# A sparse-attention decoder layer on one core: value compression's add moved to ScalarE, other PSUM banks for the v tiles, two loads moved in the program

## The chip, the core and the metric

The kernel runs on one core of one Trainium2 chip. The core has a matrix engine (TensorE, in the profile PE, with its weight loads as PEld), a vector engine (VectorE, DVE), an activation engine (ScalarE, ACT), a general engine (GpSimd, POOL) and an engine that issues transfers (SyncE, SP). Each works through its own instructions in the order in which they stand, and they meet at semaphores. The metric is the time of one run on the device, in microseconds (us); less is better.

## What is computed

One decoder layer on 1024 tokens of width 1024, in float32: a mixer with eight sparse-attention heads (two key/value heads) and eight gMLP groups, then a SwiGLU block. What matters here is the compressed branch of the attention. Overlapping blocks of 32 tokens get a position added and go through a small two-layer network; the change touches this for the values:

```python
def compress_tokens(t, pos_emb, w1, w2):
    ...
    blocks = jnp.concatenate([chunks[:, :, i:i + n_cmp] for i in range(r)], axis=3)
    blocks = (blocks + pos_emb).reshape(B, G, n_cmp, CMP_BLOCK * dh)
    return jax.nn.gelu(blocks @ w1) @ w2
...
kc = compress_tokens(heads_kv(k_c), cmp_pos_k, cmp_w1_k, cmp_w2_k)
vc = compress_tokens(heads_kv(v_c), cmp_pos_v, cmp_w1_v, cmp_w2_v)
...
mixed = jnp.concatenate([nsa_out, gm.astype(h.dtype)], axis=-1)
return jnp.einsum("bse,ed->bsd", mixed, w_out)
```

The softmax uses `exp`, the small network `gelu`; `gm` is the output of the gMLP groups, which the output projection `w_out` reads beside the attention's output.

## The kernel before

Every float32 product is made of three matmuls in a rounded format: an operand is kept as a high part (`...h`, `whi`, `bh`) and a low part (the rest, `...l`, `wlo`, `bl`), and `mm3` (L182 to L185) adds high x high, high x low and low x high. So each operand costs a rounding copy and a subtraction before TensorE may read it.

The program runs in stages: input norm and gMLP (to about 165 us of the span), projections of q, k and v with the two compressions (to about 263 us), attention over eight tiles of 128 queries, from tile 7 down to tile 0, in each of which four pairs of heads are worked on and the previous tile's output projection is slipped in (to about 590 us), then SwiGLU, whose products are nearly all matmul (to the end).

Around the change, one after the other in the program:

- `compress_in` (L414) transposes the positions into `posT` (L418, L420), makes the 16 high parts `bh` (L426) and the 16 low parts `bl` (L427), all on VectorE, from the projected values `U`, and adds up 48 matmuls in PSUM tile `ps_p` (L435), three for each of 16 slices. ScalarE applies gelu (L438) and leaves `chid`. `compress_out` (L441) transposes `chid`, splits it into `chidT`, multiplies by the second weights into `ps_p` again and leaves `vch` (L464 on ScalarE, L465 on VectorE).
- `v_proj` (L482) makes the eight tiles of v and of the gates, 24 matmuls of 280 columns each; ScalarE (L489) and VectorE (L490, L491) then empty the PSUM tile. Its bank is chosen by `turn("vproj", "wpt")`: the tiles come in the program as 4, 5, 6, 7, 0, 1, 2, 3 and get w, p, t, w, p, t, w, p. There is one bank each of w, x and p, two of a and three of t. Bank p is that of the compression too.
- Between them `wo_early` (L523) loads five 512 KB pieces of `w_out` by SP and splits them (L167 on ScalarE, L173 on VectorE). The bias table `B` (1.1 MB, L508) is loaded into the space of `bh` and `bl`, so after the last compression matmul; the 20 small `qr` loads (L571, q of a pair of heads, split by POOL at L171 and L173) follow it on SP.
- In the attention, logits of a pair of heads go to banks a and x (L673, L674), VectorE adds the bias and takes the minimum (L678, L682), ScalarE applies exp (L721).
- `output_proj` (L595) reads `gmh`, the gMLP output of a tile in its two parts: two loads of 256 KB issued by POOL (L601) from `gm_scr`, which the gMLP stage wrote long before. There is one buffer.

The instructions are not put in order by hand: a scheduler orders each engine's list by its own estimate of times and by priorities (`tc.high_priority`), within what data, buffers and banks allow. A change of a bank or of an engine so moves instructions in its neighbourhood.

Of the kernel before, what the change touches and what calls it, by code (L numbers as in the profile page):

```python
# [10 lines left out]
F32R = mybir.dt.float32r  # L11
BF16 = mybir.dt.bfloat16
AF = mybir.ActivationFunctionType
ALU = mybir.AluOpType
# [3 lines left out]
P = 128  # L18
# [8 lines left out]
NCMP = 63  # L27
# [43 lines left out]
def trunk_kernel(ctx, tc, x, rel_bias, norm_mix_pre, norm_mix_post, norm_ffn_pre, norm_ffn_post, w_in,  # L71
# [3 lines left out]
    nc = tc.nc  # L75
    x = x[0]
    out = out[0]
# [7 lines left out]
    def close(g):  # L85
        if isinstance(g, Ring):
            for p, _ in g.stack[::-1]:
                close(p)
        else:
            g.__exit__(None, None, None)  # L90
# [22 lines left out]
    def turn(key, tags):  # L113
        n = turns.get(key, 0)
        turns[key] = n + 1
        return bank(tags[n % len(tags)])

    def bank(tag):
        return psp[tag][1].tile([P, 512], F32, name="ps_" + tag)
# [15 lines left out]
    act_warm = const.tile([P, 1], F32, name="act_warm")  # L135
# [5 lines left out]
    def fl(ap):  # L141
        return ap.bitcast(F32)
# [39 lines left out]
    def mm3(ps, sh, sl, mh, ml, first, last):  # L182
        nc.tensor.matmul(ps, sh, mh, start=first, stop=False)  # L183
        nc.tensor.matmul(ps, sh, ml, start=False, stop=False)  # L184
        nc.tensor.matmul(ps, sl, mh, start=False, stop=last)  # L185

    q_scr = dram.tile([H, DH, S], F32, name="q_scr")
    gm_scr = dram.tile([2, NT, P, 4, P], F32, name="gm_scr")
# [18 lines left out]
    def xT(t):  # L207
        ts = slice((t % 4) * P, (t % 4 + 1) * P)
        return xh[t // 4][:, :, ts], xl[t // 4][:, :, ts]
# [161 lines left out]
    ps = bank("p")  # L371
# [21 lines left out]
    bh = bhlpool.tile([P, 16, G, 64], F32R, name="bh")  # L393
# [17 lines left out]
                nc.vector.tensor_tensor(kt_[g][64:128, cs], src, fl(kt_[g][0:64, cs]), op=ALU.subtract)  # L411
        return f

    def compress_in(w1, pos):  # L414
        pn = cmpool.tile([16, P], F32, name="pos_nat", bufs=2)
        nc.scalar.dma_start(out=pn, in_=pos[0].rearrange("(kt jj) d -> kt (jj d)", jj=2))
        ps = bank("t")
        nc.tensor.transpose(ps[:, :16], pn, ident[:16, :16])  # L418
        posT = cmpool.tile([P, 16], F32, name="posT", bufs=2)
        nc.vector.tensor_copy(posT, ps[:, :16])  # L420
        nc.gpsimd.memset(bh[:, :, :, 63:64].bitcast(F32), 0.0)
        nc.gpsimd.memset(bl[:, :, :, 63:64].bitcast(F32), 0.0)
        uv = U.rearrange("p g (n j) -> p g n j", j=16)
        for kt in range(16):
            src = uv[:, :, kt // 8:kt // 8 + NCMP, 2 * (kt % 8)]
            nc.vector.tensor_scalar(bh[:, kt, :, :NCMP], src, posT[:, kt:kt + 1], None, op0=ALU.add)  # L426
            nc.vector.scalar_tensor_tensor(bl[:, kt, :, :NCMP], src, posT[:, kt:kt + 1], fl(bh[:, kt, :, :NCMP]),  # L427
                                           op0=ALU.add, op1=ALU.subtract)
        w1v = w1[0].rearrange("(kt p) c -> p kt c", p=P)
        ps = bank("p")  # L430
        for q4 in range(4):
            h_, l_ = wload(w1v[:, 4 * q4:4 * q4 + 4, :])
            for c in range(4):
                kt = 4 * q4 + c
                mm3(ps[:, :256], bh[:, kt].rearrange("p a b -> p (a b)"), bl[:, kt].rearrange("p a b -> p (a b)"),  # L435
                    h_[:, c, :], l_[:, c, :], kt == 0, kt == 15)
        hid = cmpool.tile([P, 256], F32, name="chid", bufs=1)
        nc.scalar.activation(hid, ps[:, :256], AF.Gelu_apprx_tanh)  # L438
        return hid

    def compress_out(hid, w2, which):  # L441
        ps = bank("t")
        for c in range(2):
            nc.tensor.transpose(ps[:, c * P:(c + 1) * P], hid[:, c * P:(c + 1) * P], ident)
        hT = cmpool.tile([P, 2, 2, P], F32R, name="chidT", bufs=1)
        split(hT[:, 0], hT[:, 1], ps[:, :256].rearrange("p (a b) -> p a b", b=P))
        w2r = cmpool.tile([P, 2, DH], F32, name="w2r", bufs=1)
        nc.scalar.dma_start(out=w2r, in_=w2[0].rearrange("(k p) d -> p k d", p=P))
        w2s = cmpool.tile([P, 2, 2, DH], F32R, name="w2s", bufs=1)
        split(w2s[:, 0], w2s[:, 1], w2r)  # L450
        ps = bank("p")
        if which == "k":
            for c in range(2):
                mm3(ps[:64, :P], w2s[:, 0, c, :], w2s[:, 1, c, :], hT[:, 0, c, :], hT[:, 1, c, :], c == 0, c == 1)
            for g in range(G):
                src = ps[0:64, 64 * g:64 * g + 64]
                nc.scalar.copy(kt_[g][0:64, 0:64], src)
                nc.vector.tensor_tensor(kt_[g][64:128, 0:64], src, fl(kt_[g][0:64, 0:64]), op=ALU.subtract)
        else:
            for c in range(2):  # L460
                mm3(ps[:, :DH], hT[:, 0, c, :], hT[:, 1, c, :], w2s[:, 0, c, :], w2s[:, 1, c, :], c == 0, c == 1)
            for g in range(G):
                src = ps[64 * g:64 * g + 64, 0:DH]
                nc.scalar.copy(vch[0:64, g, 0:DH], src)  # L464
                nc.vector.tensor_tensor(vch[0:64, g, DH:], src, fl(vch[0:64, g, 0:DH]), op=ALU.subtract)  # L465
# [15 lines left out]

    def v_proj(vw, tiles):  # L482
        for t in tiles:
            ps = turn("vproj", "wpt")
            for k in range(KD):
                mm3(ps[:, :280], xT(t)[0][:, k, :], xT(t)[1][:, k, :], vw[k][0], vw[k][1], k == 0, k == KD - 1)
            src = ps[:, :256].rearrange("p (a d) -> p a d", d=DH)
            dst = vt[:, t].rearrange("p b g c -> p (b g) c")
            nc.scalar.copy(dst[:, :, 0:DH], src)  # L489
            nc.vector.tensor_tensor(dst[:, :, DH:], src, fl(dst[:, :, 0:DH]), op=ALU.subtract)  # L490
            nc.vector.tensor_copy(gates[:, t, :], ps[:, 256:280])  # L491
# [4 lines left out]
    proj_t(C_VC, evac_u)  # L496
    compress_out(chk, cmp_w2_k, "k")
    proj_t(C_KW, evac_k(64 + S))
    chv = compress_in(cmp_w1_v, cmp_pos_v)
    close(g_bhl)  # L500
    g_bc, bcp = pool("bc", 1, "right")
    B = bcp.tile([P, H, BW], F32, name="B")
# [27 lines left out]
            wo[k] = (hi, lo)  # L530

    v_proj(vw, (4,))
    compress_out(chv, cmp_w2_v, "v")
    v_proj(vw, (5,))
    wo_early(2)
    v_proj(vw, (6,))
# [15 lines left out]
    at = {}  # L552
# [24 lines left out]
    TILES = [7, 6, 5, 4, 3, 2, 1, 0]  # L577
# [14 lines left out]
    WO0, WO1, WON, WOE = 1, 5, 2, nc.gpsimd  # L592
    PRE = (1, 1)

    def output_proj(i):  # L595
        mixh, mixl = wout_args.pop(i)
        if not bc:
            load_bc()
        gmh = at["late"].tile([P, 2, 4, P], F32R, name="gmh", bufs=1)
        for hl in range(2):  # L600
            nc.gpsimd.dma_start(out=gmh[:, hl], in_=gm_scr[hl, i])  # L601
        xt = at["late"].tile([P, D], F32, name="xt", tag="xt", bufs=1)
        nc.sync.dma_start(out=xt, in_=x[i * P:(i + 1) * P, :])
        s2 = small.tile([P, 2], F32, name="s2o")
        h1 = at["late"].tile([P, D], F32, name="h1", tag="h1", bufs=1)
        for nh in range(2):
            ps = bank("w") if i > LX else turn("opj", "wx")
            cs = slice(nh * 512, (nh + 1) * 512)
            for k in range(KD):
                kk = (k + 4) % 8  # L610
                sh, sl = (mixh[:, kk], mixl[:, kk]) if kk < 4 else (gmh[:, 0, kk - 4], gmh[:, 1, kk - 4])
                mm3(ps, sh, sl, wo[kk][0][:, cs], wo[kk][1][:, cs], k == 0, k == KD - 1)
            nc.scalar.activation(h1[:, cs], ps, AF.Square, accum_out=s2[:, nh:nh + 1])
            nc.scalar.copy(h1[:, cs], ps)
        ss = small.tile([P, 1], F32, name="ss")
        nc.vector.tensor_tensor(ss, s2[:, 0:1], s2[:, 1:2], op=ALU.add)
        r = rstd_of(ss, D, RMS_EPS)
        for nh in range(2):
            cs = slice(nh * 512, (nh + 1) * 512)
            nc.vector.scalar_tensor_tensor(h1[:, cs], h1[:, cs], r, bc["post"][:, cs], op0=ALU.mult, op1=ALU.mult)  # L620
            nc.vector.tensor_tensor(h1[:, cs], h1[:, cs], xt[:, cs], op=ALU.add)
        nc.sync.dma_start(out=h1_scr[i], in_=h1)
        return h1, xt
# [15 lines left out]
    for ti, i in enumerate(TILES):  # L639
# [5 lines left out]
        for g in range(G):  # L645
            for pr in range(2):
                if (g, pr) == OPJ and ti > 0:
                    with tc.high_priority(HO):
                        pend = output_proj(TILES[ti - 1])
                if (g, pr) == PRE and ti > 0:  # L650
                    with tc.high_priority(HF):
                        pre_ffn(TILES[ti - 1], *pend)
# [9 lines left out]
                with tc.high_priority(HP0 if at_ < 4 else HP if i >= 4 else HP2):  # L662
                    for hh in range(2):
# [23 lines left out]
                        for c0, c1 in A_CHUNKS[i]:  # L687
                            ps = logits(c0, c1)
# [15 lines left out]
                        for c0, c1 in wch:  # L704
                            ps = logits(w0 + c0, w0 + c1)
# [14 lines left out]
                        for br, (c0, c1, col) in enumerate(((0, 64, 0), (64, na, scol), (na, na + nw, wcol))):  # L720
# [6 lines left out]
                                               op0=ALU.max, op1=ALU.mult)  # L727
                nc.vector.reciprocal(wts, wts)  # L728
                with tc.high_priority(HS):
                    for br, (c0, c1) in enumerate(((0, 64), (64, na), (na, na + nw))):  # L730
                        for hh in range(2):
                            nc.gpsimd.tensor_scalar(pts[hh][:, c0:c1], pts[hh][:, c0:c1], wts[:, hh, br:br + 1], 1.0,  # L732
                                                    op0=ALU.mult, op1=ALU.mult)
                with tc.high_priority(HV):
# [4 lines left out]
                    for gi, grp in enumerate(groups):  # L739
                        wd = 256 * len(grp)  # L740
                        ps = bank("t")
# [471 lines left out]
```

## Time and profile before

| | us |
|---|---|
| median of 3 runs | 1246.94 (1246.73 to 1247.27) |
| the profiled execution, its own time | 1244.0 |
| its span in the trace | 1242.3 |
| TensorE busy | 1195.7, 96% of the span |
| VectorE, ScalarE, GpSimd busy | 913.2, 567.2, 382.5 |

The profile shows one execution. Busy time of TensorE counts a matmul from its start to its modelled end, and matmuls overlap; how fast the stream goes is read from the distance between the starts of neighbours. Where TensorE is late, the table of waits names the engine whose signal came last. The granted clock (PEclk) is a share of full speed: 1.00 is 2.4 GHz, 0.50 is 1.2 GHz, and a value between is a stretch that had some of both.

### The profile page before, as it was taken

The page shows a single profiled execution, that of the slowest core. Times are in us where ns is not written, and L with a number is a line of the kernel's source. Part 1 is how long each engine was busy: PE and PEld are TensorE (multiplying, and loading weights), DVE is VectorE, ACT ScalarE, POOL GpSimd, SP SyncE. Part 2 cuts the span into 40 slices and gives each one's busy share as a digit, 9 for nine tenths or more (in the row PEclk, how much of TensorE's full clock was granted, in tenths as well). Part 3 has the DMA queues.
Part 4 walks back from the last instruction along what each step waited for, and adds up shares of the span by engine and source line. Part 5 has one row for each costly group of instructions (what it writes and reads, how often), then busy time and mean ns, then how long its engine had stood idle before and what let it go on. Part 6 is the DMA issues. An engine that isn't in the chain of part 4 may idle for free. (4 is left out here: it accounts for less than half of the span.)

```text
span 1242.3 us, 18159 instructions
## 1 busy us (share of the span) xinstructions
PE 1195.7 (96%) x6074; PEld 1006.9 (81%) x6074; DVE 913.2 (74%) x2037; ACT 567.2 (46%) x1254; POOL 382.5 (31%) x454
## 2 busy tenths in 40 slices
PE   6999999889999999998999999999999999999997
PEld 5888878778888988886777888888888888888885
DVE  5656337659898896877589878776787747588996
ACT  4423021257777886876544332233332324544452
POOL 3315112146545545561070222210222201132341
PEclk9999999999999999999999999999999999999999
DMA  7313454331021222425404323323233189332335
GB/s 251 95 57 96 136 170 126 104 96 35 27 64 46 63 69 68 146 71 159 156 34 150 108 104 128 111 77 110 96 117 127 62 292 348 121 111 86 96 117 203
DMA packets 106229, 143.86 MB, mean 116 GB/s; under 512 B 8120, under 2 KB 64792, under 8 KB 106136
## 3 DMA queue, kind: packets, MB, share of 16 engines
q1 hardware_dynamic: 99552, 133.43, 32.8%
q0 software_dynamic: 2304, 4.20, 1.2%
q10 hardware_dynamic: 4280, 5.08, 1.2%
q8 instruction: 48, 0.79, 0.3%
q14 instruction: 45, 0.37, 0.1%
HBM read 103.60 MB, written 40.71 MB: 116 GB/s over the span
## 5 line engine op out<-in xcount | busy, mean ns | idle before, releaser
L732 POOL TENSOR_SCALAR L<-L,wts 128x64 f32<-128x64 f32 (+8 forms) x192 | 108.4, 589 | 97.6 <-DVE wts L728 61.3
L966 DVE TENSOR_TENSOR cc<-fb,cc 128x512 f32<-128x512 f32 x140 | 94.2, 686 | 55.2 <-PE fb L185 54.5
L721 ACT ACTIVATE L<-L,mm 128x64 f32<-128x64 f32 (+8 forms) x192 | 116.3, 608 | 26.6 <-DVE mm L678 26.1
L847 POOL TENSOR_TENSOR cc<-sil 128x512 f32<-128x512 f32 x22 | 35.2, 1599 | 287.9 <-issue 225.6
L173 DVE TENSOR_TENSOR pl<-ps_t,ph 128x512 fp32r<-128x512 f32 (+1 forms) x160 | 100.6, 643 | 12.7 <-ACT ph L167 11.3
L167 ACT CAST op<-s 128x512 fp32r<-128x512 f32 x80 | 49.5, 622 | 120.9 <-PE fb L185 105.8
L184 PE MATMUL fb<-wdo,hido 128*128 128x512 f32 x264 | 102.7, 389 | 0.0
L183 PE MATMUL fb<-wdo,hido 128*128 128x512 f32 x264 | 101.9, 389 | 0.0
L185 PE MATMUL fb<-wdo,hido 128*128 128x512 f32 x264 | 100.4, 389 | 0.0
L184 PE MATMUL fb<-b_b,op 128*128 128x512 f32 x256 | 99.6, 389 | 0.0
L185 PE MATMUL fb<-b_b,op 128*128 128x512 f32 x256 | 99.4, 389 | 0.0
L183 PE MATMUL fb<-b_b,op 128*128 128x512 f32 x256 | 99.3, 389 | 0.0
L167 ACT CAST ph<-ps_t 128x512 fp32r<-128x512 f32 (+1 forms) x160 | 85.0, 555 | 30.8 <-PE ps_t L744 16.4
L744 PE MATMUL ps_t<-ident,L 128*128 128x128 f32 x592 | 89.6, 275 | 4.8 <-DVE pl L173 3.9
L173 DVE TENSOR_TENSOR hido<-hidr,hido 128x512 fp32r<-128x512 f32 x77 | 60.9, 801 | 27.8 <-ACT hido L167 27.7
L744 PEld LDWEIGHTS ps_t<-ident,L 128*128 128x128 f32 x592 | 69.1, 141 | 14.3 <-issue 5.3
L167 ACT CAST hido<-hidr 128x512 fp32r<-128x512 f32 x77 | 47.4, 620 | 66.8 <-DMA hidr<-hid_scr 25.5
L1045 POOL TENSOR_TENSOR tt<-wdr 128x512 f32<-128x512 f32 x22 | 36.1, 1646 | 134.6 <-DVE wdo L173 80.0
L167 ACT CAST op<-wraw 128x512 fp32r<-128x512 f32 x60 | 37.1, 622 | 84.9 <-PE fb L185 73.7
L173 DVE TENSOR_TENSOR op<-s,op 128x512 fp32r<-128x512 f32 x80 | 63.8, 803 | 14.1 <-ACT op L167 13.4
L753 PE MATMUL ps_p<-pl,vt 128*128 128x256 f32 x264 | 73.3, 303 | 0.5 <-DVE pl L173 0.5
L751 PE MATMUL ps_p<-ph,vt 128*128 128x256 f32 x264 | 68.5, 283 | 0.0
(399 smaller groups left out, 3466.0 us busy)
## 6 DMA issues: line engine op xcount, KB each, us to landing
wraw<-in_w_gate_up_dram SPq DMA_DIRECT2D x40, 512.0 KB, 3.6
hidr<-hid_scr SPq DMA_DIRECT2D x77, 256.0 KB, 2.7
hid_scr<-sil SPq DMA_DIRECT2D x44, 256.0 KB, 2.0
wdr<-in_w_down_dram SPq DMA_DIRECT2D x44, 256.0 KB, 5.2
hid_scr<-cc SPq DMA_DIRECT2D x33, 256.0 KB, 2.1
xt<-in_x_dram SPq DMA_DIRECT2D x16, 512.0 KB, 3.7
raw<-in_w_in_dram SPq DMA_DIRECT2D x16, 512.0 KB, 4.4
gm_scr<-gmt SPq DMA_DIRECT2D x16, 256.0 KB, 2.6
```

The costliest lines, as they stand in the source:

```text
L167: nc.scalar.copy(hi, src)
L173: e.tensor_tensor(lo, src, fl(hi), op=ALU.subtract)
L183: nc.tensor.matmul(ps, sh, mh, start=first, stop=False)
L184: nc.tensor.matmul(ps, sh, ml, start=False, stop=False)
L185: nc.tensor.matmul(ps, sl, mh, start=False, stop=last)
L721: nc.scalar.activation(L[:, c0:c1], L[:, c0:c1], AF.Exp, bias=mm[:, col:col + 1], scale=-1.0, accum_out=sums[:, hh, br:br + 1])
L732: nc.gpsimd.tensor_scalar(pts[hh][:, c0:c1], pts[hh][:, c0:c1], wts[:, hh, br:br + 1], 1.0, op0=ALU.mult, op1=ALU.mult)
L744: nc.tensor.transpose(ps[:, (bi * 2 + hh) * P:(bi * 2 + hh + 1) * P], pts[hh][:, c0:c0 + P], ident)
L751: nc.tensor.matmul(pv[:, :256], v, ph[:, bi * 256:(bi + 1) * 256], start=(gi == 0 and bi == 0), stop=False)
L753: nc.tensor.matmul(pv[:, :256], v, pl[:, bi * 256:(bi + 1) * 256], start=False, stop=last)
L966: nc.vector.tensor_tensor(dst, ps, y_, op=ALU.add)
L1045: eng.tensor_tensor(dst, x_, y_, op=op)
```

## The change

Four edits. The high parts of the value compression's operand are made by ScalarE, as an activation that adds the position (`Identity` with a bias), and no more by VectorE; the key compression stays as it was. Right behind that compression a one-column `exp` is put on ScalarE, on a spare tile. The v tiles get the banks w, t, t, x, w, t, t, p in turn, and the second half of the value compression a higher priority. The loads of `gmh` stand further ahead in the program: the first before the attention, each next one behind the output projection that used the buffer.

```diff
-    def compress_in(w1, pos):
+    def compress_in(w1, pos, on_act=False):
...
         for kt in range(16):
             src = uv[:, :, kt // 8:kt // 8 + NCMP, 2 * (kt % 8)]
-            nc.vector.tensor_scalar(bh[:, kt, :, :NCMP], src, posT[:, kt:kt + 1], None, op0=ALU.add)
+            if on_act:
+                nc.scalar.activation(bh[:, kt, :, :NCMP], src, AF.Identity, bias=posT[:, kt:kt + 1])
+            else:
+                nc.vector.tensor_scalar(bh[:, kt, :, :NCMP], src, posT[:, kt:kt + 1], None, op0=ALU.add)
...
-            ps = turn("vproj", "wpt")
+            ps = turn("vproj", "wttxwttp")
...
-    chv = compress_in(cmp_w1_v, cmp_pos_v)
+    chv = compress_in(cmp_w1_v, cmp_pos_v, True)
+    nc.scalar.activation(act_warm, chv[:, 0:1], AF.Exp)
...
-    compress_out(chv, cmp_w2_v, "v")
+    with tc.high_priority(200):
+        compress_out(chv, cmp_w2_v, "v")
...
+    gms = {}
+
+    def load_gm(i):
+        gms[i] = at["late"].tile([P, 2, 4, P], F32R, name="gmh", bufs=1)
+        for hl in range(2):
+            nc.gpsimd.dma_start(out=gms[i][:, hl], in_=gm_scr[hl, i])
+
+    load_gm(TILES[0])
+
     def output_proj(i):
...
-        gmh = at["late"].tile([P, 2, 4, P], F32R, name="gmh", bufs=1)
-        for hl in range(2):
-            nc.gpsimd.dma_start(out=gmh[:, hl], in_=gm_scr[hl, i])
+        gmh = gms.pop(i)
...
                     with tc.high_priority(HO):
                         pend = output_proj(TILES[ti - 1])
+                        load_gm(i)
```

VectorE's list from the positions of the value compression on, before (`kt_1421`, `kt_1422` are the keys of the two heads, `ps_x` the bank of the last key projection):

```order
L420 COPY posT<-ps_t 128x16
L426 TENSOR_SCALAR bh<-U,posT 128x2x63 x6
L427 SCALAR_TENSOR_TENSOR bl<-U,posT,bh 128x2x63
L426 TENSOR_SCALAR bh<-U,posT 128x2x63
L427 SCALAR_TENSOR_TENSOR bl<-U,posT,bh 128x2x63
L411 TENSOR_TENSOR kt_1421<-ps_x,kt_1421 64x512
```

and after (L430 is before's L427, L493 its L490):

```order
L420 COPY posT<-ps_t 128x16
L173 TENSOR_TENSOR wlo<-raw,whi 128x1024
L411 TENSOR_TENSOR kt_1421<-ps_x,kt_1421 64x512
L430 SCALAR_TENSOR_TENSOR bl<-U,posT,bh 128x2x63 x16
L411 TENSOR_TENSOR kt_1422<-ps_x,kt_1422 64x512
L493 TENSOR_TENSOR vt<-ps_w,vt 128x4x64
```

The sixteen `bh` have left the list, the sixteen `bl` stand together, and a split of `w_out` and one key copy now stand ahead of them, the second key copy behind them.

ScalarE's list over the same place, before:

```order
L410 CAST kt_1421<-ps_x 64x512
L489 CAST vt<-ps_w 128x4x64
L410 CAST kt_1422<-ps_x 64x512
L167 CAST whi<-raw 128x1024
L489 CAST vt<-ps_w 128x4x64
L167 CAST whi<-raw 128x1024
L438 ACTIVATE chid<-ps_p 128x256
```

and after (L441 is before's L438):

```order
L410 CAST kt_1421<-ps_x 64x512
L427 ACTIVATE bh<-U,posT 128x2x63 x16
L410 CAST kt_1422<-ps_x 64x512
L492 CAST vt<-ps_w 128x4x64
L167 CAST whi<-raw 128x1024 x2
L441 ACTIVATE chid<-ps_p 128x256
L510 DMA MW<-in_window_edge_dram 128x128
L503 ACT_TABLE_LOAD
L503 ACTIVATE act_warm<-chid 128x1
L492 CAST vt<-ps_x 128x4x64
L167 CAST chidT<-ps_t 128x256
```

The sixteen `bh` come ahead of everything that empties the v tiles, and the load of the exponential's table, which before stands ahead of the attention's first exp (L721), now stands right behind gelu.

TensorE's list where the second half of the compression is over (`xTh_155` and `xTl_156` belong to tiles 4 to 7, `xTh_150` and `xTl_151` to tiles 0 to 3), before:

```order
L184 MATMUL ps_t<-wlo,xTh_150 128x280
L185 MATMUL ps_t<-whi,xTl_151 128x280
L185 MATMUL ps_w<-whi,xTl_151 128x280
L183 MATMUL ps_p<-whi,xTh_155 128x280
L184 MATMUL ps_p<-wlo,xTh_155 128x280
```

and after:

```order
L184 MATMUL ps_t<-wlo,xTh_155 128x280
L185 MATMUL ps_t<-whi,xTl_156 128x280
L184 MATMUL ps_w<-wlo,xTh_150 128x280
L185 MATMUL ps_w<-whi,xTl_151 128x280
L183 MATMUL ps_w<-whi,xTh_150 128x280
```

Before, a tile in bank p (tile 5) follows here; after, tile 0 in bank w. Bank p then comes up for tile 3 alone, the last one, with nearly all logits of the first pair of heads ahead of it.

POOL's list at the first load of `gmh`, before:

```order
L171 TENSOR_SCALAR qt<-qr 128x256
L601 DMA gmh<-gm_scr 128x512 x2
L173 TENSOR_TENSOR qt<-qr,qt 128x256
L161 TENSOR_SCALAR whi<-wo_raw 128x1024
L732 TENSOR_SCALAR L<-L,wts 128x64 x2
```

and after (L605 is before's L601, L745 its L732):

```order
L171 TENSOR_SCALAR qt<-qr 128x256
L605 DMA gmh<-gm_scr 128x512 x2
L173 TENSOR_TENSOR qt<-qr,qt 128x256
L161 TENSOR_SCALAR whi<-wo_raw 128x1024
L745 TENSOR_SCALAR L<-L,wts 128x64 x2
```

Nothing has moved: all eight pairs of these loads stand at the same place of POOL's list as before. On SP the one difference is that `B` stands ahead of the fourth piece of `w_out`, which before went ahead of it. In the first products of SwiGLU some matmuls and splits change places as well; from the attention's second pair of heads to there the lists are the same row by row.

## Rows read from the trace of the kernel before

**Rows 1.** The page's first part: busy us (share of span) of each engine.
```profile
PE 1195.7 (96%) x6074; PEld 1006.9 (81%) x6074; DVE 913.2 (74%) x2037; ACT 567.2 (46%) x1254; POOL 382.5 (31%) x454
```

**Rows 2.** Busy time by stretch; the first line names the columns.
```profile
core 0: us, PE busy (x) PEld busy (x) DVE busy (x) ACT busy (x) POOL busy (x), PEclk, DMA share, GB/s
700.00:800.00 100.00, 100.00 (x443) 82.81 (x442) 78.80 (x112) 32.79 (x55) 17.12 (x11) 1.00 0.29 99
...
217.57:263.20 45.63, 39.61 (x270) 36.76 (x269) 27.58 (x88) 14.99 (x30) 5.23 (x9) 0.96 0.24 76
...
246.00:252.00 6.00, 5.50 (x29) 5.47 (x30) 1.33 (x8) 0.74 (x3) 1.51 (x3) 0.72 0.20 56
270.00:276.00 6.00, 5.04 (x24) 4.72 (x25) 2.42 (x9) 2.93 (x8) 6.00 (x6) 0.72 0.26 77
...
650.00:660.00 10.00, 7.66 (x31) 5.56 (x31) 10.00 (x14) 4.72 (x8) 3.20 (x2) 1.00 0.68 201
```

**Rows 3.** Waits of TensorE from 217 to 264 us: total, times, longest.
```profile
PE ps_p L183 <- DVE vch L465: 2.4, 1, 2.4
PE ps_p L185 <- DVE bl L427: 1.7, 5, 0.9
PE ps_p L183 <- DVE gates L491: 1.0, 1, 1.0
```

**Rows 4.** TensorE in order of time: start, duration, instruction [idle before <-releaser].
```profile
220.80 0.28 PE L183 MATMUL ps_p<-whi,bh 128*128 128x256 f32 x1
...
227.55 0.28 PE L183 MATMUL ps_p<-whi,bh 128*128 128x256 f32 x1
...
228.74 0.28 PE L184 MATMUL ps_p<-wlo,bh 128*128 128x256 f32 x1
...
246.50 0.36 PE L183 MATMUL ps_p<-whi,xTh 128*128 128x280 f32 x1 [2.45 <-DVE vch L465]
...
250.24 0.72 PE L673 MATMUL ps_a<-kt,qt 128*128 128x448 f32 x2
...
259.99 0.29 PE L184 MATMUL ps_p<-wlo,xTh 128*128 128x280 f32 x1
...
262.57 0.30 PE L183 MATMUL ps_p<-whi,xTh 128*128 128x280 f32 x1
...
263.20 0.37 PE L673 MATMUL ps_a<-kt,qt 128*128 128x448 f32 x1
...
270.96 0.71 PE L183 MATMUL ps_w<-whi,gmh 128*128 128x512 f32 x1 [2.23 <-DMA gmh<-gm_scr]
```

**Rows 5.** ScalarE in order of time.
```profile
218.30 0.57 ACT L410 CAST kt<-ps_x 64x512 fp32r<-64x512 f32 x1
...
242.47 1.05 ACT L167 CAST whi<-raw 128x1024 fp32r<-128x1024 f32 x1 [4.97 <-DMA raw<-in_w_out_dram]
...
252.13 1.28 ACT L721 ACT_TABLE_LOAD   x1 [5.37 <-issue]
...
255.32 1.15 ACT L721 ACTIVATE L<-L,mm 128x1024 f32<-128x1024 f32 x1 [0.33 <-DVE mm L678]
...
258.89 0.35 ACT L721 ACTIVATE L<-L,mm 128x64 f32<-128x64 f32 x1
```

**Rows 6.** VectorE in order of time.
```profile
220.75 0.68 DVE L411 TENSOR_TENSOR kt<-ps_x,kt 64x512 fp32r<-64x512 f32 x1
...
226.85 1.45 DVE L427 SCALAR_TENSOR_TENSOR bl<-U,posT,bh 128x126 fp32r<-128x126 f32 x4
...
228.76 1.22 DVE L173 TENSOR_TENSOR wlo<-raw,whi 128x1024 fp32r<-128x1024 f32 x1
```

**Rows 7.** SyncE's queue (SPq) in order of time.
```profile
233.35 0.38 SPq L508 DMA_DIRECT2D B<-s_scr  x1
...
235.84 0.33 SPq L526 DMA_DIRECT2D raw<-in_w_out_dram  x1
```

**Rows 8.** GpSimd in order of time.
```profile
243.00 0.41 POOL L171 TENSOR_SCALAR qt<-qr 128x256 fp32r<-128x256 f32 x1 [8.67 <-DMA qr<-q_scr]
```

## The prediction

> **What bounds the kernel now.** I read the page's busy shares first, then busy time by stretch, then TensorE's waits in the stretch of the change, then each engine in order of time there. TensorE is busy for 96% of the span [rows 1], VectorE for 74%. Between 700 and 800 us, and in the same way to the end, TensorE is at 100.00 at full clock [rows 2]: nothing is given back there, so the end moves by what TensorE gains or loses ahead of it. From the second pair of heads to SwiGLU the four lists read the same row by row before and after, and no instruction there has to wait for a fixed moment; so I treat the program from 263.20 on, where the second pair's first logits start [rows 4], as a block that moves as one piece. What counts is the 45.63 us from 217.57 to 263.20.
>
> How much of them is work? An undisturbed v matmul comes every 0.129 us (259.99 to 262.57 are 20 steps), a compression matmul every 0.119 us (227.55 to 228.74 are 10) [rows 4]. The stretch holds 8 tiles x 24 = 192 of the first, 24.8 us, and 48 of the second, 5.7 us. The first pair's logits are 2 x 3456 columns; at 0.129 us for 280 columns that is 3.2 us. Some ten small matmuls of the second half I estimate at 0.7 us. Sum 34.4, so 11.2 us are lost. About 0.6 of it is the first matmul of each tile, which starts a little late in either kernel; 10.6 can go.
>
> Where are they? **3.4** in the compression: its first 39 matmuls start between 220.80 and 228.74, 7.94 us, where 38 x 0.119 = 4.5 would do; the waits table names `bl` for it (the 1.7 is idle time alone) [rows 3, 4]. **2.5** where tile 5, in bank p, waits for `vch` [rows 3, 4]. **1.7** of half clock: behind that wait the granted clock was 0.72 over 6 us, so 0.28 x 6 [rows 2]. **1.0** for a bank that VectorE empties through `gates` [rows 3]. The other 2.0 are gaps of under half a us between 230 and 263, most where logits wait for VectorE or for the exponential, which is behind its table load (1.28 us at 252.13) [rows 5].
>
> **The change, part by part.** *The add on ScalarE.* VectorE now makes `bh` and `bl` one after the other for 16 slices, with key copies and `w_out` splits between them; TensorE eats a slice in 3 x 0.119 = 0.357 us. After, only `bl` is left: 1.45 us for four, 0.36 each [rows 6], just TensorE's pace. So the start decides. ScalarE is free of the key copy at 218.87 [rows 5]. A biased activation of 126 columns isn't in the trace. Bounds: an activation of 64 columns took 0.35 and one of 1024 took 1.15 [rows 5], so 0.83 ns a column and 0.35 to 0.40 us for 126 (less from start to start, if neighbours overlap). I take 0.40, worked out from the nearest row, the 64-column one: 16 end by 225.3. VectorE first does a split, 1.22 us, and a key copy, 0.68 us [rows 6], both free to start by 218.4, so until 220.3, and its first `bl` is out at 220.7. TensorE wants the first `bl` at 221.03 and the last at 226.4; VectorE gives the last at 226.5 at worst. The 3.4 go. Cover: 0.3 us; each 0.02 us that a `bl` or a `bh` takes over 0.36 costs 0.3 us in all.
>
> The Trainium skill, "ScalarE: Activation LUTs", section "Rules for kernel authors", speaks against this edit: an add belongs on VectorE, not on ScalarE. The same page, section "What ACT_TABLE_LOAD costs", gives a biased activation as some 280 ns + 0.833 ns an element with 93 ns of overlap, by which I estimate 0.29 us apart and 4.7 us for 16. By the rule's price the sum stays as it is, since here VectorE is the engine that TensorE waits for, even if ScalarE takes longer for the same add.
>
> Behind the sixteen on ScalarE now stand a key copy, tile 4's copy, two `whi` and gelu, behind the sixteen on VectorE the second key copy, until about 227.2. Tile 7, now in bank x, waits for that key copy: a new wait, 0 to 0.7 us, I take **-0.3**.
>
> *The banks and the priority.* After the compression TensorE does tile 7 (3.1 us), the transposes of `chid`, tiles 5 and 6 and the second half, tile 0 up to its 18th matmul, and then the first logits: 226.8 + 3.1 + 0.3 + 6.6 + 2.3 = 239.1, against 250.24 before [rows 4], of which 2.6 is order alone. Bank p is now wanted by tile 3 alone, at about 248, and `vch` is out by 239: the 2.5 go, and with them the half clock behind them, 1.7, as TensorE no longer stands still before it. If `vch` came 9 us later, the wait would be back.
>
> *The table.* It loads behind gelu, at about 228.4, for 1.28 us. What stands behind it, tile 7's copy and `chidT`, is only wanted when TensorE is through tile 7, at 229.9: free, and at worst 1.3 us. The 1.0 and the 2.0 of gaps go with it for the larger part, because the banks now have 6 to 10 us between emptying and use; I count all of it, and nothing of it as the bad end.
>
> *B and q.* Sooner logits need `B` and `qt` sooner. `B` goes out when the last compression matmul is over, 233.35 before [rows 7], 226.8 after. q arrived at 243.00 [rows 8], 9.65 us behind that; so 236.4, and with two POOL operations `qt` at 237.7: 1.4 us ahead of 239.1.
>
> *The loads of `gmh`.* POOL's list is the same. The wait of 2.23 us at 270.96 and the half clock behind it (0.72 from 270 to 276) [rows 2, 4] stay: **0**.
>
> *SwiGLU's start.* From 650 to 660 VectorE is busy for 10.00 of 10 us and TensorE for 7.66 [rows 2]. Seven or eight matmuls of 512 columns (8 x 0.23 = 1.8 us, by columns) have moved into that hole. Bounds 0, if they only displace others, and 1.6; no reason for either, so **0.8**.
>
> Sum: 10.6 - 0.3 + 0.8 = 11.1. The profiled execution took 1244.0 (span 1242.3) and becomes 1232.9; the median of the runs, 1246.94, becomes **1235.8**.
>
> **The rivals.** *A, q comes no sooner.* `qr` also needs its own transfers, and these now stand behind `B` and two pieces of `w_out` of 512 KB; if the queue and not `B`'s issue sets 243.00, the first logits can't start before 244.2: 5.1 us of a standing TensorE and about 1.6 of half clock behind it, as after the 2.45 us wait [rows 2, 4]. 1235.8 + 6.7 = 1242.5. For it: the 8.67 us that POOL waited [rows 8]; against: a good part of that is `B`'s own megabyte.
>
> *B, the gating tile does come sooner.* If POOL reaches its `gmh` issue earlier relative to TensorE, up to 2.2 of wait and 1.7 of clock go: 1231.9. Against: same list, and POOL moves with `qt`.
>
> *C, slower.* ScalarE works in order, and between the emptying of tiles 5 and 6 now stand the `whi` of the two last pieces of `w_out`, which are sent behind `B`. Before, ScalarE waited 4.97 us for such a piece, which came 6.63 us after its issue (235.84 to 242.47) [rows 5, 7]. After, the last one goes out at about 229.5 and should land at 236.1, and TensorE would stop for a held bank at about 244. A loss greater than the gain needs it to land after 254, 25 us behind its issue; at 30 it would be 1251. Nothing in the trace is that late, but the new order behind `B` isn't in it.
>
> *D, taken back.* The edits work, but the block from 263.20 on doesn't move as one: something in the attention that runs on its own clock (q loads, POOL's splits) is late instead, and nearly all is given back: 1245.
>
> **How the numbers follow.** Forecast 0.66, A 0.12, B 0.08, D 0.08, C 0.06. The forecast's own range is 1234 to 1239.8: up by 2.5 if none of the small gaps go, by 0.7 for bank x, by 0.8 if SwiGLU gives nothing; down by the other 0.8 and 0.6 of first matmuls. With B and most of A it is 1231 to 1242. About 0.2% either way (1244.4 to 1249.4) is what a measurement of this kernel can tell from no change: the forecast, A and B are faster, 0.86; D is the same, 0.08; C is slower, 0.06.
>
> **What would show it.** In the trace after: no wait for `bl` from 220 to 227 and 48 matmuls in 5.7 us; `bh` on ScalarE under 0.40 us; no wait for `vch`; the first logits at about 239 and a granted clock of 1.00 ahead of them; the second pair's at about 252.9; the 2.2 for `gmh` as before; from 650 to 660 (less the shift) up to 1.6 us more of TensorE. Wrong it would be if `qt` or a piece of `w_out` ends TensorE's wait ahead of the first logits, if `bl` still does in the compression, or if the second pair starts at 253 and the end has not moved with it.

## The result and the profile after

The changed kernel takes 1233.44 us in the median (1232.29 to 1233.77), the kernel before beside it 1246.84: ratio 0.9892, 95% interval 0.9875 to 0.9909. The forecast was 1235.8, within 1231 to 1242, faster. The profiled execution took 1233.15 with a span of 1231.3; the span before, 1242.3, less the 11.1 of the forecast's sum is 1231.2.

Busy time by stretch in the changed kernel. The first two lines below the names of the columns answer to the 45.63 us and the 6 us of [rows 2], the third to 270 to 276 with what lies ahead of it, the fourth shows how full VectorE is behind that, the last two answer to 700 to 800 and to the start of SwiGLU:

```profile
core 0: us, PE busy (x) PEld busy (x) DVE busy (x) ACT busy (x) POOL busy (x), PEclk, DMA share, GB/s
218.38:253.56 35.18, 35.03 (x269) 34.79 (x269) 23.98 (x72) 21.67 (x47) 5.26 (x9) 1.00 0.34 110
240.00:252.00 12.00, 12.00 (x90) 11.94 (x89) 7.74 (x36) 4.92 (x13) 2.35 (x4) 1.00 0.12 35
253.56:275.00 21.44, 19.45 (x124) 16.47 (x122) 19.75 (x77) 15.15 (x36) 19.98 (x24) 1.00 0.37 115
264.00:300.00 36.00, 33.56 (x241) 30.55 (x240) 35.08 (x118) 26.36 (x62) 25.46 (x31) 1.00 0.15 45
700.00:800.00 100.00, 100.00 (x443) 82.80 (x442) 77.48 (x107) 30.92 (x51) 19.45 (x12) 1.00 0.34 116
640.00:650.00 10.00, 8.25 (x27) 6.02 (x28) 10.00 (x14) 4.16 (x8) 2.17 (x2) 0.83 0.76 235
```

From the first v matmul to the first logits of the second pair now 35.18 us pass instead of 45.63, with TensorE busy for 35.03 of them at full clock: 10.45 us are back. TensorE in order of time, to be held against [rows 4]:

```profile
218.38 0.40 PE L183 MATMUL ps_w<-whi,xTh 128*128 128x280 f32 x1
...
221.60 0.28 PE L183 MATMUL ps_p<-whi,bh 128*128 128x256 f32 x1
...
227.23 0.28 PE L185 MATMUL ps_p<-whi,bl 128*128 128x256 f32 x1
227.66 0.37 PE L183 MATMUL ps_x<-whi,xTh 128*128 128x280 f32 x1
...
240.57 0.55 PE L686 MATMUL ps_a<-kt,qt 128*128 128x448 f32 x2
...
253.56 0.37 PE L686 MATMUL ps_a<-kt,qt 128*128 128x448 f32 x1
...
259.96 0.49 PE L183 MATMUL ps_w<-whi,gmh 128*128 128x512 f32 x1 [0.87 <-DMA gmh<-gm_scr]
```

The 48 compression matmuls start in 5.63 us, 0.120 apart, with no wait in them. The one wait that the change brings is that for bank x, 227.23 to 227.66: 0.43 where 0.12 would do. The first v matmul itself stands 0.81 us later than before (218.38 against 217.57). That delay is there from the first 11 us on, where the two programs have the same lists on all engines, and so is not the change's doing; from here on shifts are counted from the first v matmul.

ScalarE, VectorE, SyncE's queue and GpSimd in the same stretch:

```profile
219.57 6.61 ACT L427 ACTIVATE bh<-U,posT 128x126 fp32r<-128x126 f32 x16
...
229.38 1.28 ACT L503 ACT_TABLE_LOAD   x1
...
234.81 1.05 ACT L167 CAST whi<-raw 128x1024 fp32r<-128x1024 f32 x1 [3.04 <-DMA raw<-in_w_out_dram]
...
251.32 0.36 ACTq L147 DMA_DIRECT2D gpost<-in_norm_mix_post_dram  x1
```

```profile
221.20 5.58 DVE L430 SCALAR_TENSOR_TENSOR bl<-U,posT,bh 128x126 fp32r<-128x126 f32 x16
```

```profile
227.54 0.38 SPq L512 DMA_DIRECT2D B<-s_scr  x1
```

```profile
237.89 0.41 POOL L171 TENSOR_SCALAR qt<-qr 128x256 fp32r<-128x256 f32 x1 [9.37 <-DMA qr<-q_scr]
```

A `bh` comes every 0.413 us, a `bl` every 0.349. The table loads at 229.38 while TensorE is in tile 7. The split of `qt` that starts at 237.89 is over at 239.1, 1.4 us ahead of the first logits.

### The profile page after: what moved, and what is told of

It reads as the page before. It is cut to its first block, busy times and chain, and to the rows that moved or that the text cites. A ratio compares the mean times of both kernels' runs of the same rounds, so it can differ in the third digit from the quotient of the medians.

```text
span 1231.3 us, 18167 instructions
## 1 busy us (share of the span) xinstructions
PE 1190.5 (97%) x6074; PEld 1004.2 (82%) x6074; DVE 913.6 (74%) x2021; ACT 573.8 (47%) x1271; POOL 379.8 (31%) x454
## 4 chain that ended last, share of the span: by engine, by line
PE 84%; DVE 8%; ACT 3%; DMA 3%; issue 2%; POOL 0%; SPq 0%; DVEq 0%; POOLq 0%; ACTq 0%
PE fb L185 16%; PE fb L184 16%; PE fb L183 16%; PE ps_t L757 3%; PE ps_a L183 3%; PE ps_a L185 3%; PE ps_a L184 3%; PE ps_w L183 3%; PE ps_w L184 3%; PE ps_w L185 3%; PE ps_p L764 2%; PE ps_p L766 2%; DVE pl L173 2%; PE ps_x L183 2%; PE ps_x L184 1%
## 5 line engine op out<-in xcount | busy, mean ns | idle before, releaser
L745 POOL TENSOR_SCALAR L<-L,wts 128x64 f32<-128x64 f32 (+8 forms) x192 | 108.0, 585 | 98.0 <-DVE wts L741 67.2
L757 PEld LDWEIGHTS ps_t<-ident,L 128*128 128x128 f32 x592 | 68.8, 140 | 15.4 <-issue 6.1
```

Source lines behind the costliest of these rows:

```text
L757: nc.tensor.transpose(ps[:, (bi * 2 + hh) * P:(bi * 2 + hh + 1) * P], pts[hh][:, c0:c0 + P], ident)
```

## The experiments

All times below are counted as said, from the first v matmul of each kernel, as the shift against the kernel before: of the first logits, of the last v matmul, of the fifth tile (the start of the first `RECIPROCAL wts` there on VectorE, 446.27 before) and of the last matmul. They come from the time-ordered rows of each trace. u_ is the changed kernel with one edit undone, o_ the kernel before with one edit alone. The rows were not all measured at the same time; each ratio is to the kernel before as it ran beside that row.

| kernel | first logits | last v | fifth tile | end | median us | ratio (95%) |
|---|---|---|---|---|---|---|
| changed | -10.5 | -10.4 | -11.8 | -11.8 | 1233.44 | 0.9892 (0.9875 to 0.9909) |
| u_add | -3.1 | -7.4 | -11.0 | -10.9 | 1235.06 | 0.9912 (0.9897 to 0.9926) |
| u_bank | -9.9 | -7.9 | -14.5 | -13.5 | 1230.46 | 0.9866 (0.9853 to 0.9880) |
| u_gm | -10.4 | -10.4 | -10.4 | -9.4 | 1234.44 | 0.9897 (0.9882 to 0.9912) |
| gm_own | -10.4 | -6.9 | -13.3 | -13.1 | 1232.13 | 0.9889 (0.9870 to 0.9907) |
| after_again (changed) | -10.5 | -10.4 | -11.3 | -10.1 | 1234.67 | 0.9915 (0.9895 to 0.9935) |
| o_add | -10.0 | -8.0 | -14.5 | -13.6 | 1230.78 | 0.9885 (0.9862 to 0.9907) |
| o_bank | -3.4 | -7.7 | -11.1 | -11.0 | 1234.12 | 0.9913 (0.9893 to 0.9932) |
| bank_own | -9.9 | -5.6 | -11.2 | -10.1 | 1234.00 | 0.9908 (0.9887 to 0.9929) |
| one_p | -10.5 | -8.1 | -12.1 | -10.5 | 1234.82 | 0.9916 (0.9903 to 0.9929) |
| one_w | -10.5 | -6.9 | -9.4 | -8.6 | 1234.83 | 0.9915 (0.9902 to 0.9928) |
| four_p | -12.7 | -0.9 | -4.6 | -6.2 | 1239.95 | 0.9954 (0.9941 to 0.9967) |

**The adds back on VectorE (u_add).**

```diff
-    chv = compress_in(cmp_w1_v, cmp_pos_v, True)
+    chv = compress_in(cmp_w1_v, cmp_pos_v)
```

> The changed kernel with the value compression's adds put back on VectorE, the rest kept. If the ScalarE add carries the 3.4 us of the compression (so the forecast), the gaps on bl come back, about 3 us, and the time is about 3 us above the changed kernel (ratio to the kernel before about 0.992). If the new banks and the order alone do it, since a tile in bank x can be slipped in while VectorE works, it is within 1 us of the changed kernel (0.989 to 0.990).

The waits for `bl` are back, and a new one for `chid`:

```profile
PE ps_t L447 <- ACT chid L441: 1.3, 1, 1.3
PE ps_w L183 <- DMA gmh<-gm_scr: 1.0, 1, 1.0
PE ps_p L185 <- DVE bl L430: 0.9, 4, 0.3
PE ps_x L183 <- DVE kt L411: 0.5, 1, 0.5
```

The first logits come 7.3 us later than in the changed kernel, and at the fifth tile 0.8 us of that is left (against the other execution of the changed kernel, 0.3). In time it is 1.6 us from the first measurement of the changed kernel and 0.4 from the second. So the ScalarE add isn't worth its 3.4 us once the banks are there. (u_add and o_bank also reach the first v matmul 1.75 and 1.5 us later than the kernel before, which the shifts leave out and the times hold; the last section has where.)

**The old banks (u_bank).**

```diff
-            ps = turn("vproj", "wttxwttp")
+            ps = turn("vproj", "wpt")
```

> The changed kernel with the old turn of banks w, p, t, the rest kept. The forecast put 2.5 us (the wait for vch) + 1.7 (clock behind it) + part of 1.0 on banks and priority together: if the banks carry these, the time rises by 4 to 5 us (ratio 0.992 to 0.993). The rival: once the adds are on ScalarE the second half is through early and bank p is free when it is wanted anyway; then only waits between neighbours in bank p are left, at most 1 us (0.989 to 0.990).

Both expectations missed: it is faster than the changed kernel, by 2.7 us at the fifth tile. The wait for `vch` isn't there: `vch` is out 22.2 us behind the first v matmul, and a v tile takes bank p at 23.5. What is left of waits between 217 and 300 us, all of it:

```profile
PE ps_w L183 <- DVE gates L494: 0.7, 1, 0.7
PE ps_p L183 <- DVE gates L494: 0.7, 2, 0.4
PE ps_a L686 <- DVE L L695: 0.6, 2, 0.4
PE ps_x L686 <- DVE wts L741: 0.5, 1, 0.5
PE ps_p L766 <- DVE pl L173: 0.3, 1, 0.3
```

**The gating loads back (u_gm).**

```diff
-    load_gm(TILES[0])
...
-        gmh = gms.pop(i)
+        load_gm(i); gmh = gms.pop(i)
...
-                        load_gm(i)
```

> The changed kernel with the loads of gmh back where they were in the program. Every engine's list is the same, only what gmh's and gpost's space waits for is swapped: gpost (512 KB) waits for a v matmul again, as before the change. If gpost's transfer out of the way is what made gmh land 1.5 us sooner, the wait for gmh is back at about 2.2 us with half clock behind it, and of the 2.9 us some 1.3 reach the end (+1.3 us). If gmh landed sooner for another reason, the time is the same within 0.3 us and the wait stays at 0.9.

The profile showed the wait at 2.34 us again, and the fifth tile 1.4 us later. By itself that speaks for the first theory; the changed kernel itself, run again (after_again), takes it back. `gpost` was issued early there too (250.40), and yet the wait is long. The longest waits of TensorE from 217 to 300, first in the first execution of the changed kernel, then in after_again:

```profile
PE ps_t L757 <- DVE pl L173: 2.1, 1, 2.1
PE ps_w L183 <- DMA gmh<-gm_scr: 0.9, 1, 0.9
PE ps_a L686 <- DVE L L695: 0.6, 2, 0.3
```

```profile
PE ps_w L183 <- DMA gmh<-gm_scr: 2.3, 1, 2.3
PE ps_a L686 <- DVE L L695: 0.6, 2, 0.3
PE ps_t L757 <- DVE pl L173: 0.3, 1, 0.3
```

So the two halves of `gmh` took 5.9 and 5.8 us from issue to landing in one execution of the program and 7.3 and 7.8 in another, with nothing else changed. 0.5 of the 1.4 us at the fifth tile lies between two executions of one program; the 0.9 that is left doesn't show in time (1234.44 against 1233.44 and 1234.67). So the edit is worth nothing that can be seen.

The two executions also show what the wait is worth here. The longer wait and the half clock behind it put after_again 2.9 us behind at the logits that start at 266.07 in the first execution and at 268.07 in after_again. Then TensorE of the first execution stands still for VectorE, first below; in after_again, second below, it hardly does. From there on 0.5 of the 2.9 is left.

```profile
279.42 0.63 PE L757 MATMUL ps_t<-ident,L 128*128 128x128 f32 x4 [2.09 <-DVE pl L173]
```

```profile
278.98 0.63 PE L757 MATMUL ps_t<-ident,L 128*128 128x128 f32 x4 [0.30 <-DVE pl L173]
```

> The changed kernel itself, beside the next three on the same chip, as the measure for them: 1233 to 1234 us, ratio 0.989, and in the trace the second pair's work 11.8 us sooner than before, counted from the first v matmul.

**gmh in a pool of its own (gm_own).** In the kernel before, the changed kernel and u_gm, GpSimd issues the load right behind a `qt` split that has long waited for the first pair's logits; the place of the load in the source has not moved it. In the changed kernel:

```profile
253.56 0.40 POOL L171 TENSOR_SCALAR qt<-qr 128x256 fp32r<-128x256 f32 x1 [10.14 <-PE ps_a L687]
254.04 1.32 POOL L605 DMA_DIRECT2D gmh<-gm_scr  x2
```

The idea was that the space of `gmh`, free only with the last v matmuls, holds the load there. That isn't shown: in o_bank, below, the load goes out at 250.74, 6.2 us ahead of the last v matmul.

```diff
-    g_k, kp = pool("kp", 1, "right")
+    g_gm0, gmp0 = pool("gmp0", 1, "right"); g_k, kp = pool("kp", 1, "right")
...
-        gms[i] = at["late"].tile([P, 2, 4, P], F32R, name="gmh", bufs=1)
+        gms[i] = gmp0.tile([P, 2, 4, P], F32R, name="gmh", bufs=1)
...
-    close(g_k)
+    close(g_k); close(g_gm0)
```

> The changed kernel with gmh in a pool of its own, free from the projections on, so that GpSimd issues the first load some 50 us sooner. If the wait for gmh costs the end what TensorE loses by it, 0.9 us go, and as output-projection matmuls can now fill the gaps of 254 to 260 another 1 to 2: 2 to 3 us below the changed kernel. If VectorE, busy for 35.1 of 36 us from 264 to 300, takes it back, within 0.5 us of it.

The load goes out at 179.64 (254.04 in the changed kernel), output-projection matmuls move in among the first logits, and no wait for `gmh` is left. At the fifth tile it is 2.0 us ahead of after_again and 1.5 of the first execution: less than the 2 to 3 of one expectation, more than the 0.5 of the other. TensorE now waits 2.5 us for `pl` from 217 to 300, so VectorE takes a part back. How much of the gain shows in time is less sure (1232.13, with one of five runs at 1237.9). Nor is the gain that of the wait alone: TensorE's, VectorE's and ScalarE's lists differ from the changed kernel's up to 313 us.

**Each remedy alone (o_add, o_bank).** The kernel before, with the add on ScalarE and nothing else, and with the new turn of banks and nothing else. (The priority on the second half has no run of its own.)

```diff
-    chv = compress_in(cmp_w1_v, cmp_pos_v)
+    chv = compress_in(cmp_w1_v, cmp_pos_v, True)
```

> The kernel before with nothing but the value compression's high parts on ScalarE: old banks, table loaded at the first exp, loads of gmh where they were. If the parts of the forecast add up, it gains the compression's 3.4 us and no more: 1243.5 us. The rival, after the look without the new banks: once the adds are off VectorE the second half of the compression is early, and the wait for vch, the half clock behind it and most of the small gaps go by themselves; short of the changed kernel without its banks only by the gmh loads (1.4) and the table (0 to 1.3): 1232 to 1233.5 us.

```diff
-            ps = turn("vproj", "wpt")
+            ps = turn("vproj", "wttxwttp")
```

> The kernel before with nothing but the new turn of banks. If the parts of the forecast add up: the wait for vch (2.5), the clock behind it (1.7) and a part of the 1.0 go, the compression's 3.4 stay: 1242 us. The rival: banks and ScalarE add are two remedies for the same stretch, each good for nearly all; as without the ScalarE add (1235.1) plus the gmh loads (1.4) and the table (0 to 1.3): 1236 to 1238 us.

In both the parts don't add up and the rival is right, if the ratios are taken: 0.9885 and 0.9913 of 1246.84 would be 1232.5 and 1236.0. At the fifth tile the banks alone give 11 us, the add alone 14.5, both together 11.3 to 11.8. Run beside each other, o_add's times (1229.34 to 1231.85) lie all below those of the changed kernel (after_again, 1233.45 to 1235.31): **the add alone is the better kernel, by 3.9 us in the medians.** It also settles the other edits, with the old banks: u_bank has the table, the priority and the place of the `gmh` loads besides the add, and its lists on TensorE, VectorE, GpSimd and SyncE are those of o_add row by row. In o_add the table loads at 242.03, behind the start of the logits, and the two still agree within 0.1 us at the fifth tile. There the three edits are worth nothing together.

Where the add alone is ahead is best seen in TensorE's rows. Its loss against the undisturbed distance of its matmuls, in us, by time from the first v matmul:

| kernel | 0 to 36 | 36 to 46 | 46 to 56 | 56 to 100 | 100 to 200 |
|---|---|---|---|---|---|
| before | 10.1 | 1.9 | 6.4 | 9.1 | 16.4 |
| changed | 1.5 | 4.2 | 1.8 | 10.3 | 15.8 |
| after_again | 1.5 | 6.0 | 2.0 | 8.7 | 15.4 |
| u_add | 5.7 | 3.9 | 1.5 | 8.4 | 14.9 |
| o_add | 3.2 | 2.6 | 1.7 | 9.2 | 14.7 |

The new banks save 1.7 us in the first 36 and cost 1.6 to 3.4 in the next 10. There the changed kernel stands before `gmh` (0.9 of it in the first execution, 2.3 in the other); its list has only logits ahead of it, for which VectorE sets the pace. With the old banks the first pair of heads is through 2.9 us sooner (the first `RECIPROCAL wts`), its transposes and value products stand ahead of `gmh`, and the load lands while TensorE works on them. But by 56 us o_add has lost 7.5 us, as much as the first execution of the changed kernel (after_again 9.5), and is 2.2 ahead of it only from 56 to 200: so `gmh` isn't the whole of it. In o_add, from 253 to 275:

```profile
253.00:275.00 22.00, 21.34 (x139) 18.54 (x138) 17.72 (x75) 14.57 (x36) 19.31 (x23) 1.00 0.40 133
```

and in after_again over the same 22 us:

```profile
252.75:275.00 22.25, 18.85 (x111) 16.43 (x110) 17.50 (x70) 14.10 (x34) 20.31 (x25) 0.92 0.35 112
```

**Both together (bank_own).** The changed kernel with the old banks and with gmh's own pool, each edit as above.

> The changed kernel with the old turn of banks (1230.5 us) and with gmh in a pool of its own (1232.1 against 1233.4 alone). If the two gains stand beside each other: 1229 us. If both are the same gain, less waiting of TensorE in the first pairs of heads where VectorE sets the pace: 1230.5 us.

Neither came: it takes 1234.0 and is 3.3 us behind u_bank at the fifth tile. TensorE now waits for VectorE's work on the logits instead (from 217 to 300 2.3 us for `L` in three waits, 1.3 for `mm` in one).

**Leftover v matmuls (one_p, one_w, four_p).** My theory then was that the old banks win because v matmuls are left over as work for the time in which VectorE sets the pace.

```diff
-            ps = turn("vproj", "wttxwttp")
+            ps = turn("vproj", "wttxwppp")
```

> The changed kernel with the last three v tiles all in bank p (w, t, t, x, w, p, p, p), so that they can't run ahead of the logits: by the list 13 pairs of logits matmuls now stand ahead of the last v matmul, where the changed kernel has 10 and the one with old banks 12. If v matmuls left over as work for the time in which VectorE sets the pace are what the old banks have ahead, this comes out at or below 1230.8 us, some 14.5 us sooner than before by the trace, counted from the first v matmul (the changed kernel 11.3 to 11.8). If bank x for tile 7 or the second half's place is what costs, it stays at 11.3 to 11.8 and 1234 us.

```diff
-            ps = turn("vproj", "wttxwttp")
+            ps = turn("vproj", "wttxwwww")
```

> The changed kernel with the last four v tiles all in bank w: 15 pairs of logits matmuls ahead of the last v matmul. By the leftover theory it is the best of all, 14.5 to 16 us sooner than before by the trace, about 1230. The rival: a tile that must wait until the one ahead of it is emptied costs 0.3 to 0.7 us each, three of them, and the last tile comes too late for the first values product: no better than the changed kernel, 1233 to 1235.

```diff
-            ps = turn("vproj", "wttxwttp")
+            ps = turn("vproj", "wttxpppp")
```

> The changed kernel with the last four v tiles all in bank p. First logits stand 20 v matmuls further ahead. If these are what VectorE wants, 15 us sooner and 1230 us. If q (9.65 us behind the issue of B in the kernel before) isn't there yet, TensorE waits for it about 1 to 2 us, and for the second half in bank p about as long: 1232 to 1235 us.

The theory falls. one_p has more left over than u_bank by its list and no wait for `gmh`, and is only 0.3 to 0.7 us ahead of the changed kernel at the fifth tile; one_w, with still more, is 1.9 to 2.4 behind it. In four_p its rival is right as to the wait for `vch`, and there is more:

```profile
PE ps_t L757 <- DVE pl L173: 4.6, 3, 3.7
PE ps_p L183 <- DVE vch L468: 1.5, 1, 1.5
PE ps_w L183 <- DMA gmh<-gm_scr: 1.1, 1, 1.1
```

What stays open is the cause of the 2.7 to 3.2 us between new and old banks. The wait for `gmh` and the clock behind it can be told from the two executions of the changed kernel: 0.5. gm_own gains 1.5 to 2.0, but with other lists. The rest lies in how the lists put the first two tiles (o_add's differ from the changed kernel's up to 360 us); the lists that the scheduler made came out up to 10 us apart (four_p to o_add), and no run isolates one row of them.

## Why the prediction was right, and where it wasn't

The change took 11.0 us off the span and 11.1 were forecast. That it is so near is in part luck: 10.45 came in the stretch (10.3 forecast) and 0.2 in SwiGLU (0.8); 1.3 came between the second pair's first logits and 290 us, where nothing was forecast, and the later start of 0.81 took most of that back.

- **The 45.63 us: right.** 10.3 were forecast for the stretch, 10.45 came. With the 0.81 us taken off, the first logits are at 239.8 (forecast 239.1, before 250.24) and the second pair at 252.75 (forecast 252.9).
- **The add: its working was right, its worth wasn't** (see the last point). `bh` took 0.413 (0.40), `bl` 0.349 (0.36), TensorE waited for neither. (The 39 matmuls of the prediction's 3.4 us are 38 in the trace, which makes it 3.5.) The new wait for bank x was 0.31 (0.3). The cover was larger than I gave it: a `bh` that takes 0.05 over TensorE's pace cost nothing, since ScalarE started 1.6 us ahead of VectorE. The Trainium skill's figures ("ScalarE: Activation LUTs", "What ACT_TABLE_LOAD costs") gave 0.29 us apart by my estimate; the trace shows 0.41, and the measurement decides. VectorE took 0.33 for the same add in the kernel before: on ScalarE it is dearer by itself, and the edit still pays.
- **B and q: right.** 10.35 us from `B`'s issue to q instead of 9.65, and still 1.4 us ahead of the logits. Rival A didn't happen. The table was free: tile 7's copy, the first behind it, waited for TensorE alone.
- **gmh: 0, right within 0.5.** The wait at 259.96 was 0.87 in the profile (2.23 before, [rows 4]), with a clock of 1.00 behind it, and 2.3 in the other execution, with 0.92. Rival B's gain so did show once, but not for its reason: the load goes out 0.6 us behind the last v matmul, 0.5 before, and only landed sooner. Between the two executions it is worth 0.5.
- **SwiGLU: mis-sized.** 0.8 was forecast; from SwiGLU's first matmul to the last the changed kernel takes 640.74 us in both executions, 640.94 before: 0.2, and u_gm, with the same lists on TensorE and VectorE, takes 641.63, so even that is within what executions differ by. VectorE is busy for 10.00 of 10 us from 640 to 650, as it was in the hole before [rows 2]. The granted clock, which the forecast left out, is 0.83 there, where it was 1.00; that can cost 1.7 at most (0.17 of 10 us), and no run shows how much of the 0.8 it took. So my lower bound, 0, was near, and that the moved matmuls only displaced others is its likely reason, not a shown one. (From the fifth tile to the end after_again lost 1.2, ahead of SwiGLU; the last section has it.)
- **"A block that moves as one piece": right only from 290 on.** There the shift of the changed kernel is constant to 0.1 us (-11.78, -11.77, -11.81 at 290, 381 and 550 of the kernel before). But u_add is 7.3 us behind at the first logits and 0.8 at the fifth tile, and u_bank, 2.5 behind at the last v matmul, is 2.7 ahead. Up to 290, and up to 360 where the lists differ, VectorE and TensorE take turns in setting the pace, and a gain or loss at 253 isn't yet one at the end. The changed kernel gained 1.3 between 253.56 and 290 in one execution, 0.9 in the other.
- **The step that failed is the sharing out.** I gave 3.4 us to the add and 2.5 + 1.7 and most of 1.0 + 2.0 to banks, priority and table. Alone, the add gives 14.5 and the banks 11. They are two remedies for one stretch: with the add, the compression is over at 227, all that hangs on it (gelu, `vch`, `B`, q) is early, and bank p isn't waited for; with the banks, TensorE slips a v tile into the compression while VectorE works. The sum over the stretch came out because it was made from the stretch's work and time, not because of its parts.

## What to carry to other kernels

Price a stretch as its length less the work in it at its undisturbed pace, and take that as the most that all edits can bring within it; edits for different waits of one stretch compete for it. What follows the stretch may add or take: the add alone brought 14.5 us by the fifth tile, more than the 11.2 that the stretch had lost. Test each edit alone, and each one undone: here one of the four edits was worth more than all of them. Where a scheduler makes the lists, the edit that isn't needed still reorders what follows, and that can cost more than it saves.

## What the runs showed of the chip that was not expected

The same program's two 256 KB loads of `gmh` took 5.9 and 5.8 us in one execution and 7.3 and 7.8 in another, and a `w_out` piece of 512 KB beside them 5.6 and 8.3: a wait for a transfer in one profile isn't a constant of the program. Nor is what follows lost in full: of 2.9 us that the later landing cost by 266 us, 0.5 was left at 290.

Single executions differ by 0.8 us in the first 11 us. In u_add and o_bank the granted clock from 17 to 27 us was 0.83 (1.00 in the others), and they are 1.75 and 1.5 us late from there on, with the lists of the kernel before; why is open. At the end of the attention the two executions of the changed kernel differ by 1.0, in a wait for `ph` of 0.43 or 1.48 us: ScalarE stands before a weight load of SwiGLU (`wraw`, 2.16 or 3.17 us) that is ahead of `ph` in its list. So a profile can't tell apart edits under about 1 us in the whole span, while the shift between two marks in the attention, from 290 us on, repeats to some hundredths.
